# Gate and up products of the feed-forward layers: seven block products with sums of blocks in place of eight

## The chip, the core and the metric

One core of a Trainium2 chip runs the whole program. The metric is the device time of one execution, in microseconds (us). The kernel before was run three times: 1476.43, 1476.70 and 1477.50 us, median 1476.7 us.

## What is computed

A decoder trunk of two layers over 512 tokens of width 1024, in float32. Layer 0 mixes with a gated short convolution, layer 1 with dilated attention; each is followed by the same feed-forward block, which is where the change is. Cut to that:

```python
def swiglu(x, w_gate_up, w_down):          # w_gate_up: 1024 x 5632, w_down: 2816 x 1024
    g, u = jnp.split(x @ w_gate_up, 2, axis=-1)
    return (jax.nn.silu(g) * u) @ w_down

for layer in range(2):
    ...                                    # mixer of the layer
    h = h + rms_norm(y, mix_norm_post[layer])
    f = swiglu(rms_norm(h, ffn_norm_pre[layer]), ...)
    h = h + rms_norm(f, ffn_norm_post[layer])
```

## The kernel before

Every float32 operand of a matrix product is split into a high part (a cast on ACT, L93) and a low part (source minus high part, on DVE, L94). `split` does this. A product is then three matmuls: high times high, low times high, high times low. The weights stand in the array (128 x 128, loaded before each matmul); the activations `xh`, `xl` stream through, 512 token columns at a time (256 in a few places).

`ffn` walks through 11 chunks. A chunk takes 256 gate features and 256 up features; each of the two comes as one load of 1024 x 256 weights (1 MB) into a buffer `raw`, of which there are two. `parts` splits 128 features at a time into `wh` and `wl`, six buffers of each. A chunk is 2 x 2 tiles of 128 features, each 8 blocks of the 1024 inputs times 3 matmuls of 512 columns into one PSUM bank: `feature_mm` (L160) lets a gate tile and an up tile take turns. Afterwards ACT applies silu to the gate bank (L415) and DVE multiplies it with the up bank (L416). `down` follows: 22 blocks of the product's inputs, each 24 matmuls of 512 columns into eight PSUM banks (`y0a` to `y3b`).

The order on each engine is set by a scheduler at build time, which places the instructions of the program by its own estimate of times. Each engine then runs its list strictly in that order: an instruction that waits holds back everything behind it on the same engine. `strict` (L133) pins matmuls to the order in which the program writes them. The attention stage uses it; its products `vps` (values) are matmuls of 256 columns. PSUM has four banks of tag `mm` and four of tag `at`.

The first chunk of `ffn` also finishes the norm of the layer's input: tokens 256 to 511 of `xh` and `xl` are transposed and split during it (`pending.rest`).

Of the kernel before, what the change touches and what calls it, by code (L numbers as in the profile page):

```python
# [15 lines left out]
P = 128  # L16
# [22 lines left out]
def trunk(  # L39
# [27 lines left out]

    xp = [keep.tile([P, KT * T], F32R, name=n, align_bytes=LINE) for n in ("xh", "xl")]  # L70
# [5 lines left out]
    cst = keep.tile([P, 576], F32, name="cst")  # L76
# [5 lines left out]
    cols = keep.tile([P, 64], F32, name="cols")  # L82
    taps, gq, gkv = cols[:, 0:24], cols[:, 24:32], cols[:, 32:40]

    mhalf = keep.tile([P, 1], F32, name="mhalf")
# [2 lines left out]
    def bank(tag, name):  # L88
        return psum.tile([P, T], F32, tag=tag, name=name)
# [14 lines left out]
    def parts(src, gain=None, pool=wp, bufs=6):  # L104


        _, a, b = src.shape
        wh = pool.tile([P, a, b], F32R, tag="wh", name="wh", bufs=bufs, align_bytes=LINE)
        wl = pool.tile([P, a, b], F32R, tag="wl", name="wl", bufs=bufs, align_bytes=LINE)
        if gain is None:  # L110
            split(wh, wl, src)
            return wh, wl
        for i in range(a):
            g = gain[:, i:i + 1]
            nc.scalar.mul(wh[:, i], src[:, i], g)  # L115
            nc.vector.scalar_tensor_tensor(  # L116
                wl[:, i], src[:, i], g, wh[:, i].bitcast(F32), ALU.mult, ALU.subtract)
        return wh, wl
# [272 lines left out]
                    after.after_half(tt, n)  # L391
        return after

    def ffn(layer, pending, after):
        w = ffn_w_gate_up[layer]
        with ExitStack() as phase:
            apool = phase.enter_context(tc.tile_pool(name=f"a{layer}", bufs=4))
            act = []
            for n, bufs in ((1, NF - 12), (0, 12)):
# [3 lines left out]
                act = [pool.tile([P, T], F32, tag=f"act{k}", name="act")  # L403
                       for k in range(bufs)] + act
            for c in range(NF // 2):
                rg = load_cols(w, c * 256)
                ru = load_cols(w, DFF + c * 256)
                mg, mu = makers("mm", rg), makers("at", ru)
                rest = pending.rest() if c == 0 else {}
                if c == 1:  # L410
                    rest["marks"] = [pending.made[NT - 1]] * 4
                ps = feature_mms([mg[0], mu[0], mg[1], mu[1]], **rest)
                for j in range(2):
                    s = apool.tile([P, T], F32, tag="silu", name="s", bufs=2)
                    nc.scalar.activation(s, ps[2 * j], AF.Silu)  # L415
                    nc.vector.tensor_tensor(act[2 * c + j], ps[2 * j + 1], s, ALU.mult)  # L416
# [6 lines left out]
            return down(apool, act, ffn_w_down[layer], held_pool, after)  # L423

    def norm_pool(stack, n):

# [4 lines left out]
    with ExitStack() as phase:  # L431
# [57 lines left out]
        for c in range(KT // 2):  # L489
# [58 lines left out]
    pending = ffn(0, pending, lambda ys: Next(npool, ys, ffn_norm_post[0], None))  # L548

# [299 lines left out]
            f()  # L849

    with ExitStack() as phase:
        npool = norm_pool(phase, 1)
# [31 lines left out]
        ffn(1, pending, lambda ys: Last(npool, ys, ffn_norm_post[1], None))  # L884


_INS = ["x", "positions", "mix_norm_pre", "mix_norm_post", "ffn_norm_pre", "ffn_norm_post",
# [42 lines left out]
```

## Time and profile before

| | before |
|---|---|
| median of three runs | 1476.7 us |
| the profiled execution | 1476.04 us |
| its span, first to last instruction | 1474.3 us |
| TensorE (PE) busy | 1459.1 us, 99% of the span |
| weight loads (PEld) busy | 1247.3 us, 85% |
| DVE busy | 692.6 us, 47% |
| ACT busy | 657.8 us, 45% |
| mean granted TensorE clock | 0.996 of full speed |
| DMA | 93 GB/s on average |

The span and the profiled execution differ by 1.7 us, which lie outside the first and the last instruction. Matmuls are pipelined: a matmul's record is longer than the distance to the next one's start, so the time that a matmul costs is read from the distance of starts or from the length of an unbroken stretch, not from its mean duration.

### The profile page before, as it was taken

The numbers are of one execution on the slowest core, as the hardware profiler recorded it, in microseconds if no ns is written. First come the engines' busy times: TensorE is split into PE (matmuls) and PEld (weight loads), VectorE is DVE, ScalarE is ACT, GpSimd is POOL, SyncE is SP. The second block draws the span as 40 slices with busy tenths as digits, with TensorE's granted clock in tenths as the row PEclk, the third lists the DMA queues.
The fourth block names the chain that finished last, engine by engine and source line by source line (L and its number), as shares of the span: only waits on it lengthen the run. The fifth ranks groups of instructions, "written<-read, shape, count | busy, mean of one in ns | idle before, by whom it ended". The sixth has DMA issues, their size and how long they took to land.

```text
span 1474.3 us, 20308 instructions
## 1 busy us (share of the span) xinstructions
PE 1459.1 (99%) x8160; PEld 1247.3 (85%) x8160; DVE 692.6 (47%) x1381; ACT 657.8 (45%) x1337; POOL 57.3 (4%) x108
## 2 busy tenths in 40 slices
PE   9999999999999999999999999999999999999998
PEld 7888898888888889898899889889789888888886
DVE  5644453232223446767457555745545323223433
ACT  4313342222222336896677768768444222222321
POOL 1000100000000010010000001001010000000000
PEclk9999999999999999999999999999999999999999
DMA  6333123233232312322212312312113331332311
GB/s 217 114 116 114 57 91 107 89 114 103 83 127 102 116 56 70 125 66 92 94 46 87 111 62 60 115 58 60 58 58 115 114 110 62 114 128 94 107 57 57
DMA packets 110516, 137.44 MB, mean 93 GB/s; under 512 B 3502, under 2 KB 99286, under 8 KB 110423
## 3 DMA queue, kind: packets, MB, share of 16 engines
q1 hardware_dynamic: 108852, 135.69, 28.0%
q8 instruction: 64, 1.05, 0.3%
q0 software_dynamic: 1280, 0.26, 0.3%
q14 instruction: 30, 0.24, 0.1%
q10 hardware_dynamic: 290, 0.20, 0.0%
HBM read 133.92 MB, written 2.23 MB: 92 GB/s over the span
## 4 chain that ended last, share of the span: by engine, by line
PE 72%; issue 25%; DVE 1%; POOL 1%; ACT 1%; DMA 0%; SPq 0%; POOLq 0%; DVEq 0%; ACTq 0%
PE mmf L133 16%; PE atf L160 15%; PE mmf L160 12%; PE vps L133 10%; PE s L133 2%; PE tr L133 2%; PE o L133 2%; PE y L133 1%; PE tr L283 1%; PE y2b L231 0%; PE y3b L231 0%; PE y2b L227 0%; PE y3b L227 0%; PE y3b L229 0%; PE y2a L231 0%
## 5 line engine op out<-in xcount | busy, mean ns | idle before, releaser
L94 DVE TENSOR_TENSOR wl<-raw,wh 128x1024 fp32r<-128x1024 f32 x176 | 210.7, 1223 | 70.1 <-ACT wh L93 69.7
L93 ACT CAST wh<-raw 128x1024 fp32r<-128x1024 f32 x176 | 178.1, 1046 | 75.9 <-PE atf L160 43.1
L160 PE MATMUL atf<-xh,wh 128*128 128x512 f32 (+1 forms) x560 | 181.0, 366 | 0.0
L160 PE MATMUL atf<-xh,wl 128*128 128x512 f32 (+1 forms) x560 | 180.4, 365 | 0.0
L160 PE MATMUL atf<-xl,wh 128*128 128x512 f32 (+1 forms) x560 | 180.0, 365 | 0.0
L415 ACT ACTIVATE s<-mmf 128x512 f32<-128x512 f32 x44 | 26.3, 598 | 330.3 <-PE mmf L160 322.1
L416 DVE TENSOR_TENSOR act<-atf,s 128x512 f32<-128x512 f32 x44 | 30.4, 692 | 297.3 <-ACT s L415 297.3
L116 DVE SCALAR_TENSOR_TENSOR wl<-raw,cols,wh 128x256 fp32r<-128x256 f32 x272 | 115.8, 483 | 104.2 <-ACT wh L115 104.2
L160 PE MATMUL mmf<-xh,wh 128*128 128x512 f32 (+1 forms) x496 | 162.1, 365 | 0.6 <-ACT xh L93 0.6
L160 PE MATMUL mmf<-xl,wh 128*128 128x512 f32 (+1 forms) x496 | 160.4, 362 | 0.0
L160 PE MATMUL mmf<-xh,wl 128*128 128x512 f32 (+1 forms) x496 | 160.3, 362 | 0.0
L115 ACT ACTIVATE wh<-raw,cols 128x256 fp32r<-128x256 f32 x272 | 115.0, 498 | 65.5 <-PE mmf L133 46.9
L160 PEld LDWEIGHTS atf<-xh,wh 128*128 128x128 f32 x560 | 99.6, 189 | 16.7
L160 PEld LDWEIGHTS atf<-xh,wl 128*128 128x128 f32 x560 | 99.6, 189 | 16.8
L160 PEld LDWEIGHTS atf<-xl,wh 128*128 128x128 f32 x560 | 99.5, 189 | 16.9
L133 PE MATMUL mmf<-xh,wh 128*128 128x512 f32 x352 | 110.7, 396 | 0.0
L133 PE MATMUL mmf<-xh,wl 128*128 128x512 f32 x352 | 108.8, 390 | 0.0
L133 PE MATMUL mmf<-xl,wh 128*128 128x512 f32 x352 | 108.5, 390 | 0.0
L160 PEld LDWEIGHTS mmf<-xh,wh 128*128 128x128 f32 x496 | 88.6, 191 | 15.6 <-ACT xh L93 1.1
L160 PEld LDWEIGHTS mmf<-xl,wh 128*128 128x128 f32 x496 | 87.5, 189 | 14.4
L160 PEld LDWEIGHTS mmf<-xh,wl 128*128 128x128 f32 x496 | 87.5, 189 | 14.3
L93 ACT CAST ah<-act 128x512 fp32r<-128x512 f32 x44 | 27.1, 620 | 117.5 <-PE y3b L229 116.0
(202 smaller groups left out, 2455.8 us busy)
## 6 DMA issues: line engine op xcount, KB each, us to landing
raw<-in_ffn_w_gate_up SPq DMA_DIRECT2D x44, 1024.0 KB, 6.6
raw<-in_w_kv SPq DMA_DIRECT2D x24, 1024.0 KB, 5.2
raw<-in_ffn_w_down SPq DMA_DIRECT2D x22, 1024.0 KB, 4.8
raw<-in_w_q SPq DMA_DIRECT2D x12, 1024.0 KB, 5.1
raw<-in_conv_w_in SPq DMA_DIRECT2D x11, 1024.0 KB, 5.3
raw<-in_conv_w_out SPq DMA_DIRECT2D x4, 1024.0 KB, 4.9
raw<-in_w_o SPq DMA_DIRECT2D x4, 1024.0 KB, 5.1
h<-in_x SPq DMA_DIRECT2D x4, 512.0 KB, 7.3
```

The costliest lines, as they stand in the source:

```text
L93: return [nc.scalar.copy(hi, src).ins, nc.vector.tensor_tensor(lo, src, hi.bitcast(F32), ALU.subtract).ins]
L94: nc.vector.tensor_tensor(lo, src, hi.bitcast(F32), ALU.subtract).ins]
L115: nc.scalar.mul(wh[:, i], src[:, i], g)
L116: nc.vector.scalar_tensor_tensor(wl[:, i], src[:, i], g, wh[:, i].bitcast(F32), ALU.mult, ALU.subtract)
L133: traced[:] = [op(*args, **kwargs).ins]
L160: nc.tensor.matmul(*args, **kwargs)
L283: nc.tensor.transpose(ps[:, k, :], hn[:, c][:, k * P:(k + 1) * P], ident)
L415: nc.scalar.activation(s, ps[2 * j], AF.Silu)
L416: nc.vector.tensor_tensor(act[2 * c + j], ps[2 * j + 1], s, ALU.mult)
```

## The change

From the third chunk on, in both layers, the product of a weight matrix (1024 inputs x 256 features) with the activations (1024 inputs x 512 tokens) is cut into 2 x 2 blocks: two halves of the inputs, two tiles of 128 features, two halves of the tokens. Eight block products are needed in the plain way. The change forms sums of weight blocks and of activation blocks and gets the same result from seven block products (Winograd's form of Strassen's algorithm), then from sums of the results. A block product is 4 blocks of inputs times 3 matmuls of 256 columns (`product`).

A `Pair` is one load (256 gate or 256 up features), so a chunk is a gate pair and an up pair, and nine chunks in two layers make 36 pairs. In a pair, `parts(n1)` splits the first tile (products 1 and 2), `dh`, `dl` split a block of the second tile (product 4), four additions on DVE overwrite `raw` with sums, and two more `parts` split those (products 6, 3, 7, 5). The results go through three banks: `z` takes products 1, 6, 7 and 4 one on top of the other, and is copied out between them; `zx` takes product 2; `zy` products 5 and 3. Products 4 and 3 of a pair are issued during the next pair. In the last pair of a layer the order differs, so that all ends there.

`sums_of_x` forms the sums of the activation blocks once per layer, in the buffers of the last four `act` tiles, and splits them; one of them, for product 4, replaces a block of `xh`, `xl` in place. The norm's pool is closed during the products and opened again before `down`. `xh`/`xl` and `wh`/`wl` become halves of one tile, `x` and `w`.

The core of the diff:

```diff
-        wh = pool.tile([P, a, b], F32R, tag="wh", name="wh", bufs=bufs, align_bytes=LINE)
-        wl = pool.tile([P, a, b], F32R, tag="wl", name="wl", bufs=bufs, align_bytes=LINE)
+        w = pool.tile([P, 2 * a, b], F32R, tag="w", name="w", bufs=bufs, align_bytes=LINE)
+        wh, wl = w[:, 0:a], w[:, a:2 * a]
...
+    class Pair:
+        def __init__(self, pool, raw, xs, gate, act):
...
+            n1, n2 = raw[:, :, 0:P], raw[:, :, P:2 * P]
+            k1, k2 = slice(0, KT // 2), slice(KT // 2, KT)
...
+            a1 = parts(n1)
+            a22 = [pool.tile([P, KT // 2, P], F32R, tag="ah", name=n, align_bytes=LINE)
+                   for n in ("dh", "dl")]
+            split(*a22, n2[:, k2])
+            add(n2[:, k2], n2[:, k1], n2[:, k2])
+            add(n2[:, k1], n1[:, k1], n2[:, k1])
+            add(n1[:, k1], n1[:, k1], n2[:, k2])
+            add(n1[:, k2], n1[:, k2], n1[:, k1])
+            s1 = parts(n1)
+            s2 = parts(n2)
...
+        def p1(self):
+            self.product(self.z, 1, True, True)
+            nc.scalar.copy(self.r[:, 0:256], self.z)
+        def p2(self):
+            self.product(self.x, 2, True, True)
+            nc.vector.tensor_tensor(self.r[:, 0:256], self.x, self.r[:, 0:256], ALU.add)
+        def p6(self):
+            self.product(self.z, 6, False, True)
+            nc.scalar.copy(self.r[:, 256:512], self.z)
+        def p5(self):
+            self.product(self.y, 5, True, True)
+        def p7(self):
+            self.product(self.z, 7, False, True)
+            nc.scalar.mul(self.r2, self.z, -1.0)
+        def c22(self):
+            nc.vector.tensor_tensor(self.r2, self.r2, self.y, ALU.subtract)
...
+        def p4(self):
+            self.product(self.z, 4, False, True)
...
+        def p3(self):
+            self.product(self.y, 3, False, True)
+            nc.vector.tensor_tensor(self.r[:, 256:512], self.y, self.r[:, 256:512], ALU.add)
...
-            for c in range(NF // 2):
-                rg = load_cols(w, c * 256)
-                ru = load_cols(w, DFF + c * 256)
+            for c in range(2):
+                rg, ru = loads(c)
...
+                xs = sums_of_x(sums, act[-4:])
+                before = None
+                for c in range(2, NF // 2):
+                    gate = None
+                    for raw in loads(c):
+                        p = Pair(apool, raw, xs, gate, act[c])
+                        p.p1()
+                        if gate and c == NF // 2 - 1:
+                            before.p4()
+                            p.p6()
+                            before.p3()
+                            p.p7()
+                            p.p2()
+                            p.p5()
+                            p.c22()
+                            p.p4()
+                            p.p3()
+                            break
+                        p.p2()
+                        if before:
+                            before.p4()
+                        p.p6()
+                        if before:
+                            before.p3()
+                        p.p5()
+                        p.p7()
+                        p.c22()
+                        before = gate = p
```

On PE, a chunk of the kernel before reads like this; a gate and an up tile take turns, and every row is one matmul of 512 columns:

```order
L160 MATMUL mmf<-xh,wh 128x512
L160 MATMUL atf<-xh,wh 128x512
L160 MATMUL mmf<-xh,wl 128x512
L160 MATMUL atf<-xh,wl 128x512
L160 MATMUL mmf<-xl,wh 128x512
L160 MATMUL atf<-xl,wh 128x512
```

The same place in the changed kernel; from product 6 of one pair to product 2 of the next, the `zy<-x` row being product 3 of the pair before:

```order
L134 MATMUL z<-xs,w 128x256 x12
L134 MATMUL zy<-x,w 128x256 x12
L134 MATMUL zy<-xs,w 128x256 x12
L134 MATMUL z<-xs,w 128x256 x12
L134 MATMUL z<-x,w 128x256 x12
L134 MATMUL zx<-x,w 128x256 x12
```

Twelve matmuls of 256 columns now go into one bank in a row, and 84 of them make a pair where 48 of 512 columns did.

On ACT, at the end of a layer's second chunk, the kernel before goes on with silu and the casts of the next chunk's weights:

```order
L415 ACTIVATE s<-mmf 128x512 [waits PE_49,Activation_49]
L93 CAST wh<-raw 128x1024 [waits DMAHW4_49]
L93 CAST wh<-raw 128x1024 [waits DMAHW5_49,PE_49]
L93 CAST ah<-act 128x512 [waits DVE_49]
L415 ACTIVATE s<-mmf 128x512 [waits PE_49,Activation_49]
```

In the changed kernel the same place, where the first pair begins; the first cast is the one that replaces a block of `x`, L440 is the copy of `z` after product 1 of the first pair:

```order
L94 CAST x<-act 128x2x512 [waits PE_49]
L536 ACTIVATE s<-mmf 128x512 [waits PE_49,Activation_49]
L94 CAST w<-raw 128x1024 [waits DVE_49]
L94 CAST w<-raw 128x1024 [waits PE_49]
L440 COPY r<-z 128x256 [waits PE_49]
```

The two casts ahead of the copy are those of the second pair's sums; they stand in front of a copy that the first pair's product 6 needs.

ACT again, in the changed kernel, at the last two pairs of a layer; L455 takes product 7 of the gate pair out of `z`, the four casts are the last pair's two sums and `down`'s first two weights, L462 is a silu, L440 the copy after product 1 of the last pair:

```order
L455 ACTIVATE r_3815<-z 128x256 [waits PE_49,Activation_49]
L94 CAST w<-raw 128x1024 [waits DVE_49]
L94 CAST w<-raw 128x1024
L94 CAST w<-raw 128x1024 [waits DMAHW4_49]
L94 CAST w<-raw 128x1024 [waits Activation_49]
L462 ACTIVATE s_3908<-r_3815 128x256 [waits DVE_49]
L440 COPY r<-z 128x256 [waits PE_49]
```

In the pairs ahead of it three casts stand there, not four.

## Rows read from the trace of the kernel before

**Rows 1.** The page: span, and busy time with its share and instructions.

```profile
span 1474.3 us, 20308 instructions
PE 1459.1 (99%) x8160; PEld 1247.3 (85%) x8160; DVE 692.6 (47%) x1381; ACT 657.8 (45%) x1337; POOL 57.3 (4%) x108
```

**Rows 2.** What PE waited for: us in total, times, longest.

```profile
PE tr L133 <- DVE p L755: 3.4, 1, 3.4
PE s L133 <- DVE st L669: 1.8, 3, 0.6
PE idle L468 <- DVE u L502: 1.3, 1, 1.3
PE tr L283 <- DVE hn L272: 1.3, 2, 1.1
PE mmf L160 <- ACT xh L93: 0.6, 2, 0.3
```

**Rows 3.** Chain that ended last: start, length, unbroken matmuls (first 256 columns, second 512).

```profile
26.81 5.76 PE mmf L160 x48
49.61 10.88 PE mmf L160 x48
...
650.98 17.47 PE vps L133 x144
```

**Rows 4.** Timeline of PE: start, length; eight 256-column matmuls each into one bank.

```profile
193.78 1.12 PE L160 MATMUL mmf<-xh,wl 128*128 128x256 f32 x8
194.74 1.12 PE L160 MATMUL mmf<-xl,wh 128*128 128x256 f32 x8
```

**Rows 5.** Busy time of each engine in one chunk of layer 0.

```profile
239.58:261.30 21.72, 21.72 (x98) 17.98 (x96) 6.71 (x7) 5.48 (x7) 0.00 (x0) 1.00 0.31 98
```

**Rows 6.** Groups by line and shape: count, busy us, mean ns, idle before.

```profile
L94 DVE TENSOR_TENSOR wl<-raw,wh 128x1024 fp32r<-128x1024 f32 x176 | 210.7, 1223 | 70.1 <-ACT wh L93 69.7
L116 DVE SCALAR_TENSOR_TENSOR wl<-raw,cols,wh 128x256 fp32r<-128x256 f32 x272 | 115.8, 483 | 104.2 <-ACT wh L115 104.2
...
L133 PEld LDWEIGHTS vps<-wh,xl 128*128 128x128 f32 x384 | 59.9, 192 | 0.0
...
L755 DVE TENSOR_SCALAR p<-p,f 128x256 f32<-128x256 f32 x112 | 31.9, 352 | 0.0
...
L94 DVE TENSOR_TENSOR al<-act,ah 128x512 fp32r<-128x512 f32 x44 | 30.2, 691 | 98.0 <-ACT ah L93 98.0
L93 ACT CAST ah<-act 128x512 fp32r<-128x512 f32 x44 | 27.1, 620 | 117.5 <-PE y3b L229 116.0 <-DVE act L416 1.5
...
L741 ACT COPY v<-vps 32x256 f32<-32x256 f32 x64 | 23.2, 363 | 0.8
```

**Rows 7.** Timeline of ACT and DVE in a chunk: two casts, two subtractions back to back.

```profile
229.41 1.99 ACT L93 CAST wh<-raw 128x1024 fp32r<-128x1024 f32 x2
...
230.48 2.36 DVE L94 TENSOR_TENSOR wl<-raw,wh 128x1024 fp32r<-128x1024 f32 x2 [0.24 <-ACT wh L93]
```

**Rows 8.** DMA issues: count, KB, median us from issue to landing.

```profile
raw<-in_ffn_w_gate_up SPq DMA_DIRECT2D x44, 1024.0 KB, 6.6
raw<-in_w_kv SPq DMA_DIRECT2D x24, 1024.0 KB, 5.2
raw<-in_ffn_w_down SPq DMA_DIRECT2D x22, 1024.0 KB, 4.8
```

**Rows 9.** Timeline of ACT: the second silu of the second chunk, layers 0 and 1.

```profile
239.80 0.60 ACT L415 ACTIVATE s<-mmf 128x512 f32<-128x512 f32 x1 [7.88 <-PE mmf L160]
...
1151.95 0.60 ACT L415 ACTIVATE s<-mmf 128x512 f32<-128x512 f32 x1 [7.88 <-PE mmf L160]
```

**Rows 10.** PE's longest wait, and busy times with granted clock (1.00 is full) after it.

```profile
1045.48 1.97 PE L133 MATMUL tr<-ident,p 128*128 128x128 f32 x8 [3.37 <-DVE p L755]
...
1045.00:1050.00 5.00, 4.52 (x18) 3.93 (x19) 5.00 (x21) 1.17 (x2) 0.00 (x0) 0.66 0.63 210
```

More of the change, by code (lines that the diff above doesn't have):

```diff
@@ L75, in trunk @@
     ident = keep.tile([P, P], F32, name="ident")
-    cst = keep.tile([P, 576], F32, name="cst")
+    cst = keep.tile([P, 514], F32, name="cst")
     invf, sgn = cst[:, 0:1], cst[:, 1:2]
@@ L392, in down, with add, product @@
         return after
-    def ffn(layer, pending, after):
+    class Pair:
+        def __init__(self, pool, raw, xs, gate, act):
+            self.pool, self.xs, self.gate, self.act = pool, xs, gate, act
+            n1, n2 = raw[:, :, 0:P], raw[:, :, P:2 * P]
+            k1, k2 = slice(0, KT // 2), slice(KT // 2, KT)
+            def add(out, a, b):
+                nc.vector.tensor_tensor(out, a, b, ALU.add)
+            a1 = parts(n1)
[8 more added lines that the diff above has]
+            s2 = parts(n2)
+            self.w = {
+                1: [z[:, k1] for z in a1], 2: [z[:, k2] for z in a1],
+                6: [z[:, k1] for z in s1], 3: [z[:, k2] for z in s1],
+                7: [z[:, k1] for z in s2], 5: [z[:, k2] for z in s2], 4: a22}
+            self.z, self.x, self.y = (bank(t, n)[:, 0:T // 2] for t, n in (
+                ("mm", "z"), ("mm", "zx"), ("at", "zy")))
+            self.r = pool.tile([P, T], F32, tag="al", name="r", align_bytes=LINE)
+            self.r2 = pool.tile([P, T], F32, tag="al", name="r2", align_bytes=LINE)[:, 0:T // 2]
+        def product(self, out, n, first, last):
+            w, x = self.w[n], self.xs[n]
+            out = out.rearrange("p (t n) -> p t n", n=P)
+            for k in range(KT // 2):
+                for p in range(3):
+                    strict(nc.tensor.matmul, out, w[p == 1][:, k, :], x[p == 2][:, :, k, :],
+                           start=first and k + p == 0, stop=last and k == KT // 2 - 1 and p == 2,
+                           skip_group_check=True)
+        def p1(self):
[14 more added lines that the diff above has]
+            nc.vector.tensor_tensor(self.r2, self.r2, self.y, ALU.subtract)
+            g = self.gate
+            if g is None:
+                self.s2 = self.pool.tile([P, T], F32, tag="silu", name="s2", bufs=2)
+                nc.scalar.activation(self.s2[:, 256:512], self.r2, AF.Silu)
+            else:
+                nc.vector.tensor_tensor(
+                    self.act[:, 768:1024], self.r2, g.s2[:, 256:512], ALU.mult)
+        def p4(self):
+            self.product(self.z, 4, False, True)
+            g = self.gate
+            if g is None:
+                nc.scalar.activation(self.s2[:, 0:256], self.z, AF.Silu, scale=-1.0)
+            else:
+                nc.vector.scalar_tensor_tensor(
+                    self.act[:, 512:768], self.z, -1.0, g.s2[:, 0:256], ALU.mult, ALU.mult)
+        def p3(self):
+            self.product(self.y, 3, False, True)
+            nc.vector.tensor_tensor(self.r[:, 256:512], self.y, self.r[:, 256:512], ALU.add)
+            g = self.gate
+            if g is None:
+                self.s1 = self.pool.tile([P, T], F32, tag="silu", name="s1", bufs=2)
+                nc.scalar.activation(self.s1, self.r, AF.Silu)
+            else:
+                nc.vector.tensor_tensor(self.act[:, 0:512], self.r, g.s1, ALU.mult)
@@ new lines, in block, with sums_of_x @@
+    def block(z, k, t):
+        return z[:, 2 * t:2 * t + 2, 4 * k:4 * k + 4, :]
+    def sums_of_x(pool, scratch):
+        b11, b12, b21, b22 = (t.rearrange("p (t k n) -> p t k n", t=2, n=P) for t in scratch)
+        for out, k, t in ((b11, 0, 0), (b12, 0, 1), (b22, 1, 1), (b21, 1, 0)):
+            nc.vector.tensor_tensor(
+                out, *(block(z, k, t).bitcast(F32) for z in (xh, xl)), ALU.add)
+        nc.vector.tensor_tensor(b11, b11, b12, ALU.subtract)
+        nc.vector.tensor_tensor(b12, b22, b12, ALU.subtract)
+        nc.vector.scalar_tensor_tensor(b22, b11, -1.0, b22, ALU.mult, ALU.subtract)
+        nc.vector.scalar_tensor_tensor(b21, b22, -1.0, b21, ALU.mult, ALU.subtract)
+        homes = pool.tile([P, 6 * D], F32R, name="xs", align_bytes=LINE).rearrange(
+            "p (c e t k n) -> p c e t k n", c=3, e=2, t=2, n=P)
+        homes = [[homes[:, c, e] for e in range(2)] for c in range(3)]
+        xs = {n: [block(z, k, t) for z in (xh, xl)]
+              for n, k, t in ((1, 0, 0), (2, 1, 0), (3, 1, 1), (4, 0, 1))}
+        for n, src in ((6, b22), (5, b11), (7, b12), (4, b21)):
+            if n not in xs:
+                xs[n] = homes.pop()
+            split(*xs[n], src)
+        return xs
@@ L395, in ffn @@
+    def ffn(layer, pending, norms, after):
         w = ffn_w_gate_up[layer]
@@ L415, in ffn @@
                     nc.scalar.activation(s, ps[2 * j], AF.Silu)
-                    nc.vector.tensor_tensor(act[2 * c + j], ps[2 * j + 1], s, ALU.mult)
+                    nc.vector.tensor_tensor(
+                        act[c][:, j * T:(j + 1) * T], ps[2 * j + 1], s, ALU.mult)
+            norms.close()
+            with tc.tile_pool(name=f"sums{layer}", bufs=1, side="right") as sums:
+                xs = sums_of_x(sums, act[-4:])
[26 more added lines that the diff above has]
+                        before = gate = p
+            npool = norm_pool(norms, f"{layer}f")
             def held_pool():
@@ L421, in held_pool @@
                 return stack.enter_context(tc.tile_pool(name=f"held{layer}", bufs=2))
-            return down(apool, act, ffn_w_down[layer], held_pool, after)
+            halves = [a[:, j * T:(j + 1) * T] for a in act for j in range(2)]
+            return down(apool, halves, ffn_w_down[layer], held_pool, lambda ys: after(npool, ys))
     def norm_pool(stack, n):
```

18 lines of the change are left out of this document (11 added, 7 removed).

## The prediction

> **What bounds the kernel now.** I read the page first: PE is busy for 1459.1 of 1474.3 us [rows 1]. Then what PE waited for: five causes, 8.4 us together, none of them in the chunks that change [rows 2]. In one such chunk PE is busy for all of its 21.72 us, DVE for 6.71 and ACT for 5.48 [rows 5]. So the time is the sum of the matmuls, and the changed stretch gets shorter by what its matmuls save, until another engine can't keep up. DVE and ACT have room, but the change spends most of it.
>
> **What a matmul costs** is the distance of starts in an unbroken stretch, since the records overlap. 48 matmuls of 512 columns take 10.88 us, 48 of 256 columns 5.76 [rows 3], so 226.7 and 120.0 ns: half the columns cost 53%, not half. The change writes twelve times in a row into one bank. That costs nothing extra: eight matmuls of 256 columns into one bank start 0.96 us ahead of the next eight into it, 120 ns each [rows 4]. In a longer run, 144 in 17.47 us, it is 121.3 ns [rows 3].
>
> **Term 1, the matmuls.** A pair had 48 of 512 columns, 10.88 us; it gets 84 of 256 columns, 84 x 0.120 = 10.08 us. Eight products become seven (12.5% less), but the price of the shorter matmul takes back nearly half of that. 36 pairs x 0.80 = **28.8 us saved**. At 121.3 ns it would be 36 x (10.88 - 10.19) = 24.8.
>
> A weight load stands ahead of each of these matmuls, and its record takes 192 ns [rows 6], longer than the 120 ns from one matmul to the next; in that row of 256-column products the loads lie beside the matmuls.
>
> **Term 2, DVE and ACT inside the pairs.** DVE per pair, by mean durations [rows 6]: three subtractions of 1024 (1.223), one of 512 and four additions of 512 (0.691 each) = 7.1 us, then its sums of results. No row shows a 256-wide sum of two tiles; 0.352 and 0.483 us are the nearest on either side, and I take 0.43, halfway between, to be an estimate. A gate pair has three of these, an up pair four, one of 0.48 and one of 0.69: 1.3 and 2.9 us. A chunk is 18.4 of 20.16 us. Back to back these overlap by a tenth (two subtractions 2.36 us, two casts 1.99) [rows 7], so about 16 us. ACT needs about 11 of 20.16. Neither is the bound by its sum.
>
> What can bound is the strict order. I followed one chunk through ACT's and DVE's lists, with a pair as a slot of 10.08 us, its products each 1.44 us long and seen by the other engines 0.2 us after their last matmul began to drain. Two loops are tight. (a) At the end of a gate pair ACT takes product 7 out of `z` (at 10.28), casts the next pair's two sums and the weights after those (three casts 0.95 us apart), a silu, and only then copies product 1 of the up pair, done at 14.02 us; product 6 of that pair wants the bank at 14.40. Margin 0.4 us. (b) In the up pair the sum after product 3 waits for PE until 17.48, two additions, the same three casts, and then product 7 leaves `z` at 22.3; the next pair's product 4 wants it at 23.04. Margin 0.7 us. The last of the three casts waits for a load as well: its buffer is freed at 14.0, the cast's turn is at 21.0, and loads of this shape that run alone take 5.2 us [rows 8]; the 6.6 of the gate and up loads come from two that start together. Margin 1.8 us. So I take nothing for the inside of the pairs, and keep 0.3 us a chunk, 18 x 0.3 = 5 us, as the upper bound of what small unseen gaps make; below zero nothing is to be had, since PE is already taken as unbroken.
>
> **Term 3, the start of a layer's pairs.** The second chunk ends on PE where its last silu starts, at 239.8 us in layer 0 [rows 9]. Then ACT may cast the block that replaces one of `x` (1.05 us, to 240.9), and DVE, whose list holds the same step, subtracts (to 242.1), makes two additions (to 243.4), and only then can ACT cast the second pair's sums (to 245.3) and reach the copy of product 1 (to 245.65). Product 6 wanted `z` at 239.6 + 2.9 = 242.5. **3.2 us** of waiting. In layer 1 the second chunk ends at 1151.7, one addition less lies in the chain, and the same count gives **2.6 us**. The sums of `x` themselves (eight steps of 1.2 us and four splits, some 15 us of DVE per layer) lie beside the second chunk, 21.7 us of PE with 6.7 of DVE [rows 5]; if that cover were gone they would be late by up to their own length, but by my count they end 4 us or more ahead of the first product that reads them.
>
> **Term 4, the end of a layer's pairs.** There four casts, not three, stand ahead of the copy after the last pair's product 1, and that pair's order takes product 2 out from between: product 6 wants `z` at 12.96 instead of 14.40. The copy is done at 10.55 + 4 x 0.95 + 0.4 (silu) + 0.4 = 15.0. **2.0 us** of waiting. Later DVE, which has `down`'s first subtractions in its list, reads `zy` 0.7 us too late for product 3 of this pair. **2.7 us a layer.** After that `down` has 5.4 us of matmuls for each block and nothing on the path.
>
> **The clock.** Ahead of PE's one wait of 3.37 us it had been little busy, and in the 5 us behind the granted clock was 0.66, that is 1.7 us of full-speed time lost [rows 10]; the shorter waits of [rows 2] left none of this on the page. Four waits of 2.0 to 3.2 us come in; each may cost between 0 and 1.7 us. I take 0.8 us in all, half of one such drop, since PE is dense right up to each wait.
>
> **The sum.** 28.8 - 3.2 - 2.6 - 2 x 2.7 - 0.8 = 16.8 us. The profiled execution of 1476.04 us (span 1474.3) becomes 1459.2, and since it lies 0.7 us below the median of the runs, 1476.7, that becomes **1459.9, say 1460 us**.
>
> **The rivals.**
>
> *Nothing waits at the ends* (0.08): if the copies at the start and the end come sooner than I count them, terms 3 and 4 go and 28.8 us remain: 1448. For it: PE had almost no wait before [rows 2]. Against it: the list on ACT, where the casts stand ahead of the copy whatever they take.
>
> *The margins inside the pairs don't hold* (0.20): loops (a) and (b) have 0.4 and 0.7 us, and each strings together five or six instructions on two engines. If each of six steps costs 0.13 us more than I took, 0.8 us together, (a) is 0.4 us late and (b) 0.1: 18 x 0.5 = 9 us, so 1469; 1467 to 1473 for a little less or more. Against it: durations in the groups hardly vary, and the overlaps were read from this stage [rows 7].
>
> *The weights come too late* (0.08), the one that ends slower: with two buffers, a pair's load can start only when the pair two before has split its sums, at 14.0 in a chunk, and ACT's cast of it at 21.0 stands ahead of the step that frees `z`. The load has 1.8 us in hand over 5.2, and loop (b) 0.7 more. From a landing time of 7.7 us on, each us more is paid once per chunk, 18 times; the kernel is slower by more than 0.2%, 1479.7, from 7.7 + 19.7 / 18 = 8.8 us on. At 9.0 us it would be 18 x 1.3 = 23 us on top of 1460: 1483. Against it: 4.8 to 6.6 us in the rows [rows 8], and fewer loads at a time than before. With a landing of 8.5 to 8.8 us it would end within 0.2% (0.03).
>
> *The weight loads show* (0.01). If a load could not lie beside a matmul at 256 columns, each of the 3024 matmuls would cost up to 192 + 120 ns, 943 us in place of the 392 of before: about 2030 us. The rows speak against it: 120 ns with a load ahead of each [rows 3, 4, 6]. The Trainium skill's page "TensorE: Matmul & The Clock Gate", section "Part 3: Packing small matmuls — row/col tiling", says that weight loads overlap running matmuls only when they go to another group of rows, which full 128-row loads never do; by that rule this rival would be the forecast. The trace does not agree with it here.
>
> That the change does not do what it says I give nothing: PE's list has 3024 matmuls of 256 columns where 1728 of 512 were.
>
> **How the numbers follow.** Forecast, 0.60: 1460, with 1453 to 1467 for the bounds of the price per matmul (4 us), of the clock (up to 6 us more, 1 less) and of terms 3 and 4 (a third either way, 4 us). Margins 0.20, no waits 0.08, late weights 0.08 and 0.03, loads 0.01. The range of 1450 to 1472 leaves out most of the full gain, some of the margins' upper end, and the slow cases: 0.2. Within 0.2% means 1473.7 to 1479.7 us, about what a measurement of this kernel can tell from no change. Faster by more: 0.60 + 0.20 + 0.08 = 0.88; within: 0.03; slower: 0.08 + 0.01 = 0.09.
>
> **What would show it.** Term 1: an unbroken stretch of 12 matmuls `z` in 1.44 us, and a chunk of 20.2 us. Term 2: no wait of PE on ACT or DVE between the fourth and the tenth chunk; if loop (a) fails, PE's `z` waits for L440, if (b), for L455. Terms 3 and 4: one wait of `z` for L440 of 3.2 and 2.6 us about 3 us behind each second chunk, one of 2.0 for L440 and one of 0.7 for DVE's L458 ahead of each `down`. Clock: below 1.00 behind these waits or not. I am wrong if a chunk takes over 20.6 us, or if the loads of single pairs take longer than 7 us to land.

## The result, and the profile after

| | before | after |
|---|---|---|
| time of the runs, median (lowest to highest), us | 1476.57 (1476.35 to 1477.5), 4 runs | 1453.29 (1453.15 to 1455.22), 4 runs |
| ratio, 95% interval | | 0.9844, 0.9827 to 0.9861 |
| profiled execution, time and span, us | 1476.04, 1474.3 | 1453.27, 1451.5 |

The change saves 23.3 us, 1.6%. The forecast was 1460 with a range of 1450 to 1472: the direction and the range are right, and the time is 6.7 us lower than forecast. The page of the profile after the change, its head and its line on the loads of the gate and up weights (count, size, median us from issue to landing):

```profile
span 1451.5 us, 23433 instructions
PE 1433.4 (99%) x9456; PEld 1286.6 (89%) x9456; DVE 913.6 (63%) x1747; ACT 760.4 (52%) x1543; POOL 59.7 (4%) x108
...
raw<-in_ffn_w_gate_up SPq DMA_DIRECT2D x44, 1024.0 KB, 5.1
```

Against [rows 1], PE has 25.7 us less work and is as full as before (99%), while DVE has taken on 221 us and ACT 103. The loads land in 5.1 us where [rows 8] had 6.6. What PE waited for (us in total, times, longest), to be held against [rows 2]:

```profile
PE z L134 <- ACT r L440: 4.0, 2, 2.0
PE tr L134 <- DVE p L909: 3.4, 1, 3.4
PE s L134 <- DVE st L823: 1.8, 3, 0.6
PE idle L622 <- DVE u L656: 1.3, 1, 1.3
PE mmf L161 <- ACT x L94: 0.6, 2, 0.4
PE mmf L161 <- DVE w L95: 0.3, 1, 0.3
```

Two lines are new. `z` waits for ACT's copy L440 twice, 2.0 us each: once in each layer, at the end of its pairs. And a matmul of layer 1's first chunk waits 0.3 us for a low part of a weight. The second to the fifth line stood there before. No line tells of a wait between the first and the last pair. Two stretches of 20.16 us, from the start of layer 0's third chunk on, in the columns of [rows 5]:

```profile
240.10:260.26 20.16, 20.16 (x169) 20.13 (x168) 11.78 (x16) 10.74 (x18) 0.00 (x0) 1.00 0.16 53
260.26:280.42 20.16, 20.16 (x170) 20.16 (x170) 16.93 (x26) 10.18 (x17) 0.00 (x0) 1.00 0.32 105
```

From one pair's product 2 to that of the next pair but one it is 20.16 us in the trace, a chunk, and PE is busy for all of it, where [rows 5] had 21.72. DVE's part grew from 6.71 to 16.93, ACT's from 5.48 to 10.18.

Runs of one kernel differ by up to 4.4 us here, with the granted clock (below). Losses of 1 or 2 us are therefore read between starts of matmuls in the traces. Three stretches carry all that follows: A, from layer 0's first pair to layer 1's first chunk; B, layer 1's first two chunks; C, from layer 1's first pair to the last matmul of the program.

| kernel | median of the runs | A | B | C |
|---|---|---|---|---|
| before | 1476.57 | 865.50 | 46.66 | 315.29 |
| after | 1453.29 | 853.27 | 47.75 | 303.43 |
| x_read_late | 1455.31 | 855.41 | 47.74 | 305.57 |
| p2_back | 1450.57 | 851.85 | 47.75 | 301.95 |
| casts_late | 1451.18 | 851.72 | 47.73 | 302.16 |
| sums_late | 1454.07 | 854.73 | 46.65 | 303.67 |
| layer0_only | 1465.42 | 854.73 | B and C: 361.95 (before 361.95) | |
| pad512 | 1461.30 | 856.52 | 47.74 | 306.99 |
| pad2x512 | 1470.15 | 862.26 | 47.75 | 312.84 |
| short_p2 | 1446.59 | 849.84 | 47.75 | 300.07 |
| all3 | 1447.49 | 851.06 | 46.65 | 301.06 |

So the change gains 12.23 us in A and 11.86 in C, and loses 1.09 in B. If nothing were lost, A and C would each gain the 14.40 of 18 pairs at 0.80.

### The profile page after: what moved, and what is told of

It is laid out like the page before. It is cut to its first block, busy times and chain, and to the rows that moved or that the text cites. A ratio compares the mean times of both kernels' runs of the same rounds, so it can differ in the third digit from the quotient of the medians.

```text
span 1451.5 us, 23433 instructions
## 1 busy us (share of the span) xinstructions
PE 1433.4 (99%) x9456; PEld 1286.6 (89%) x9456; DVE 913.6 (63%) x1747; ACT 760.4 (52%) x1543; POOL 59.7 (4%) x108
## 4 chain that ended last, share of the span: by engine, by line
PE 95%; issue 2%; ACT 1%; DVE 1%; POOL 1%; POOLq 0%; DVEq 0%; ACTq 0%
PE mmf L134 17%; PE z L134 14%; PE vps L134 10%; PE atf L161 10%; PE zy L134 7%; PE mmf L161 7%; PE zx L134 4%; PE s L134 2%; PE o L134 2%; PE tr L134 2%; PE y L134 1%; PE tr L284 1%; PE y0a L230 1%; PE y1b L232 1%; PE y0a L232 1%
## 5 line engine op out<-in xcount | busy, mean ns | idle before, releaser
L95 DVE TENSOR_TENSOR w<-raw,w 128x1024 fp32r<-128x1024 f32 x212 | 251.6, 1220 | 81.7 <-ACT w L94 81.4
L94 ACT CAST w<-raw 128x1024 fp32r<-128x1024 f32 x212 | 212.7, 1046 | 107.3 <-PE atf L161 43.1
L134 PE MATMUL mmf<-x,w 128*128 128x512 f32 x1056 | 246.5, 391 | 0.0
L134 PEld LDWEIGHTS mmf<-x,w 128*128 128x128 f32 x1056 | 196.2, 188 | 39.4
L161 PE MATMUL atf<-x,w 128*128 128x512 f32 (+1 forms) x816 | 174.7, 340 | 0.0
L161 PEld LDWEIGHTS atf<-x,w 128*128 128x128 f32 x816 | 134.9, 190 | 16.8
L134 PE MATMUL vps<-w,x 128*128 128x256 f32 x1152 | 142.3, 284 | 0.0
L134 PEld LDWEIGHTS vps<-w,x 128*128 128x128 f32 x1152 | 139.0, 192 | 1.9
L161 PE MATMUL mmf<-x,w 128*128 128x256 f32 (+1 forms) x624 | 131.3, 326 | 1.0 <-ACT x L94 0.6
L134 PE MATMUL z<-xs,w 128*128 128x256 f32 x864 | 115.8, 284 | 4.0 <-ACT r L440 4.0
L161 PEld LDWEIGHTS mmf<-x,w 128*128 128x128 f32 x624 | 99.3, 191 | 11.5 <-ACT x L94 1.3
```

Of the source, the lines that this page charges most:

```text
L94: return [nc.scalar.copy(hi, src).ins, nc.vector.tensor_tensor(lo, src, hi.bitcast(F32), ALU.subtract).ins]
L95: nc.vector.tensor_tensor(lo, src, hi.bitcast(F32), ALU.subtract).ins]
L134: traced[:] = [op(*args, **kwargs).ins]
L161: nc.tensor.matmul(*args, **kwargs)
```

## The experiments

**x_read_late: when may the cast into `x` begin?** The prediction had put 5.8 us of waiting at the start of the pairs, and the profile shows none. In the trace ACT casts the block that replaces one of `x` at 234.41, well ahead of the second chunk's end at 240.10 (timeline of ACT: start, length, operation):

```profile
234.41 1.05 ACT L94 CAST x<-act 128x1024 fp32r<-128x1024 f32 x1
```

What it overwrites are the input blocks 0 to 3 of two token tiles. The chunk's matmuls go through the input blocks in order, so their last readers are done halfway through the chunk's second pair of features. The experiment reads the blocks in reverse order in that one pair.

```diff
-        todo = [(k, p) for k in range(KT) for p in range(3)]
+        todo = [(k, p) for k in (reversed(range(KT)) if late else range(KT)) for p in range(3)]
...
-                feature_mm(pairs[i:i + 2], 0, NT, attn, fill)
+                feature_mm(pairs[i:i + 2], 0, NT, attn, fill, late and i == 2)
...
-                    rest["marks"] = [pending.made[NT - 1]] * 4
+                    rest.update(marks=[pending.made[NT - 1]] * 4, late=True)
```

> The second chunk's second pair of features reads the eight input blocks in reverse order, so blocks 0 to 3 are read last, and ACT's cast of a sum of x into the place of x's blocks 0 to 3 has to wait for the chunk's end. All else is as in the changed kernel. Theory A: term 3 of the prediction was wrong in one place only, the moment from which this cast may begin (it ran at 234.41, halfway through that pair, not at 240.1). Then it must now start at about 240.3, and with it everything that stands behind it on ACT (a silu, two casts, the copy L440) comes some 1.1 to 1.3 us too late for product 6: a wait of PE of 1.1 to 1.3 us about 3 us behind each second chunk, 2.4 us in all, near 1455.7. Rival B, the chain as the prediction counted it, with DVE's subtraction and two additions in it: waits of 3.2 and 2.6 us, 5.8 in all, near 1459. Rival C, this cast does not set that copy at all: no wait, 1453.3.

Measured: the wait appears in both layers. Timelines of ACT, DVE and PE in x_read_late (in brackets the idle time ahead and what ended it); the second chunk ends at 240.32 here:

```profile
240.07 1.05 ACT L94 CAST x<-act 128x1024 fp32r<-128x1024 f32 x1 [5.22 <-PE atf L161]
...
243.40 0.37 ACT L440 COPY r<-z 128x256 f32<-128x256 f32 x1
...
236.52 1.42 DVE L407 TENSOR_TENSOR raw<-raw 128x512 f32<-128x512 f32 x2
241.15 1.23 DVE L95 TENSOR_TENSOR x<-act,x 128x1024 fp32r<-128x1024 f32 x1 [3.22 <-ACT x L94]
...
243.87 1.67 PE L134 MATMUL z<-xs,w 128*128 128x256 f32 x12 [0.51 <-issue]
```

The cast now waits for PE, and product 6 starts 0.67 us later than two products behind the chunk's end (240.32 + 2.88 = 243.20), of which the profile lists 0.51. Theory A is right in its place and nearly twice too large: the copy L440 comes 3.08 us behind the chunk's end where it came 2.41 behind it, so ACT's list moved by 0.67 and not by 1.05, because the cast overlaps the last matmuls. That all of the 0.67 shows tells that the changed kernel had no room left here. The same place there, timelines of DVE, ACT and PE:

```profile
236.00 1.22 DVE L95 TENSOR_TENSOR x<-act,x 128x1024 fp32r<-128x1024 f32 x1
237.14 1.41 DVE L407 TENSOR_TENSOR raw<-raw 128x512 f32<-128x512 f32 x2
...
242.51 0.38 ACT L440 COPY r<-z 128x256 f32<-128x256 f32 x1
...
242.99 1.67 PE L134 MATMUL z<-xs,w 128*128 128x256 f32 x12
```

The copy ends 0.10 us ahead of product 6 in both.

Rival B, the chain of the prediction, is not tested by this run. With the edit the scheduler also changed DVE's list: in the changed kernel the subtraction stands ahead of the two additions (236.00, 237.14), here behind them (241.15, 236.52). ACT's two casts of the second pair's sums read what these additions write. So with the changed kernel's own list a cast at 240.07 would have held them back; by the distances in these traces product 6 would then have come some 2.9 us late, an estimate that no run checks. That ACT does wait for this chain is seen in pad512, below. The rest of what this kernel's profiled execution lost (A +2.14, C +2.14) is the clock, below.

**p2_back and casts_late: the wait at the end of the pairs.** ACT's and PE's timeline there, in the changed kernel, layer 0:

```profile
409.20 3.87 ACT L94 CAST w<-raw 128x1024 fp32r<-128x1024 f32 x4
412.98 0.41 ACT L462 ACTIVATE s<-r 128x256 f32<-128x256 f32 x1
413.29 0.36 ACT L440 COPY r<-z 128x256 f32<-128x256 f32 x1
...
413.70 1.70 PE L134 MATMUL z<-xs,w 128*128 128x256 f32 x12 [2.01 <-ACT r L440]
415.24 1.60 PE L134 MATMUL zy<-x,w 128*128 128x256 f32 x12
```

Four casts, a silu, the copy: product 6 has to wait until `z` is read. It starts 2.16 us later than straight behind product 4; the listed 2.01 is counted from the end of the last matmul's record. Behind the wait its twelve matmuls take 1.54 us, not 1.44: a restart costs 0.1. The first experiment gives PE other work in that time, the second takes two of the four casts out of ACT's list ahead of the copy.

```diff
                         if gate and c == NF // 2 - 1:
+                            p.p2()
                             before.p4()
...
-                            p.p2()
```

> In the last pair of each layer product 2 is put back between product 1 and product 4, as in all other pairs, in place of behind product 7. Theory A: the wait of 2.0 us at the end of a layer's pairs is that of product 6 for the copy of product 1 behind four casts on ACT, so 1.44 us more of matmuls ahead of it leave 0.6 us of it: 2 x 1.44 = 2.9 us less, near 1450.4. Rival B, the casts themselves come late there because DVE's sums or down's loads are late: ACT is then later by as much, and the time stays at 1453.3. Rival C, product 2's sum on DVE now stands in another's way at the start of down: some of the 2.9 us comes back as a wait of y or zy.

Measured: A 1.42 and C 1.48 us shorter, 2.90 together against 2.9 expected; 0.57 us of the wait is left in each layer. Theory A holds.

```diff
-                pool, wk = apool, parts(raw[:, k % 2:k % 2 + 1, :])
+                with behind(copied): pool, wk = apool, parts(raw[:, k % 2:k % 2 + 1, :])
...
-            nc.scalar.copy(self.r[:, 0:256], self.z)
+            return nc.scalar.copy(self.r[:, 0:256], self.z).ins
...
-                        p.p1()
+                        copied[:] = [p.p1()]
```

> down's casts of its weights are held back until the last pair's product 1 has been copied out of z; by ACT's list two casts instead of four then stand between the copy of product 7 and the copy L440. Theory A: the four casts are the whole of the wait of 2.0 us per layer; with two fewer (0.95 us each) the copy comes 1.9 us sooner and 0.1 us of waiting is left: 2 x 1.9 = 3.8 us less, near 1449.5. Rival B: down's first matmuls then come too late, since their weights and their split of act are made two casts later, and PE waits for w at the start of down for up to 2 us: nothing gained, 1453. Rival C: as A for layer 0, but layer 1 has another limit (half, 1451.4).

Measured: A 1.55 and C 1.27 us shorter, 2.8 of the 3.8 expected. Of the 2.16 us by which product 6 came late behind L440, 0.28 are left (it starts at 412.75, straight behind product 4 it would be 412.47), too short for the list, and the next copy on the same list holds up PE too:

```profile
412.34 0.36 ACT L440 COPY r<-z 128x256 f32<-128x256 f32 x1
415.79 0.38 ACT L448 COPY r<-z 128x256 f32<-128x256 f32 x1
...
412.75 1.69 PE L134 MATMUL z<-xs,w 128*128 128x256 f32 x12
416.23 1.70 PE L134 MATMUL z<-xs,w 128*128 128x256 f32 x12 [0.35 <-ACT r L448]
```

The two casts that were held back, and two splits of `act`, now stand ahead of the copy of product 6, and product 7 waits for that. None of the three expectations had this. Down's first matmuls come in time, so rival B falls.

**sums_late: layer 1's first chunk.** B is 1.09 us longer than before, a loss that the prediction's sum doesn't have at all. In DVE's list there, two sums of `x` stand ahead of the last norm of the rows, and PE later waits for a weight (timelines of DVE, POOL and PE, changed kernel):

```profile
1094.56 2.36 DVE L494 TENSOR_TENSOR act<-x 128x1024 f32<-128x1024 f32 x2
1097.37 1.42 DVE L273 SCALAR_TENSOR_TENSOR hn<-h,y,grow 128x512 f32<-128x512 f32 x2 [0.45 <-POOL y L252]
...
1095.95 1.39 POOL L252 TENSOR_TENSOR y<-a,mhalf 128x1 f32<-128x1 f32 x1
...
1101.23 1.21 DVE L95 TENSOR_TENSOR w<-raw,w 128x1024 fp32r<-128x1024 f32 x1
...
1102.50 2.18 PE L161 MATMUL mmf<-x,w 128*128 128x256 f32 x16 [0.33 <-DVE w L95]
```

The sums end at 1096.92, and the norm (L273) then waits 0.45 us more for POOL. Beside the sums POOL's two steps ahead of the norm, L250 and L252, take 1.34 and 1.39 us by the trace, against 0.30 and 0.56 in the kernel before and in sums_late, where DVE is idle during them. So the norm is late by the sums themselves and by a slower POOL; no run separates the two.

```diff
-            nc.vector.tensor_tensor(
+            with behind(mark): nc.vector.tensor_tensor(
                 out, *(block(z, k, t).bitcast(F32) for z in (xh, xl)), ALU.add)
...
-                xs = sums_of_x(sums, act[-4:])
+                xs = sums_of_x(sums, act[-4:], pending.made[NT - 1] if layer else ())
```

> In layer 1 the four first sums of x on DVE (L494) are issued only once all of x is made, where two of them stood ahead of the last norm of the pending layer's rows. Theory A: the 1.09 us that layer 1's first chunk lost come from these two additions of 1024 ahead of the last hn and of a weight's low part; with them moved, first chunk and second chunk take 46.66 us again as before the change, 1.1 us less: 1452.2. Rival B: the loss in the first chunk has another cause (ACT's casts of the sums, the shape of the start) and stays: 1453.3. Rival C: the sums then end too late for the products that read them at the start of the pairs, and PE waits there for xs: more than 1453.3.

Measured: B is 46.65 us, where 46.66 was before the change; theory A holds for this stretch, and nothing waits for the sums later. The runs are not faster (1454.07, 1452.2 expected). In the profiled execution the clock fell behind the wait at layer 0's end, which took 1.46 us in A; why the other three (1453.71 to 1454.32) are no faster, no trace tells. The 1.1 us are shown by the stretch B alone.

**layer0_only: do the layers touch each other?**

```diff
-            for c in range(2):
+            for c in range(NF // 2 if layer else 2):
...
-                xs = sums_of_x(sums, act[-4:])
+                xs = None if layer else sums_of_x(sums, act[-4:])
-                for c in range(2, NF // 2):
+                for c in range(2, 2 if layer else NF // 2):
```

> Block products in layer 0 alone; layer 1 runs its eleven chunks as before the change. Theory: the layers don't touch each other. Layer 0 keeps its gain of 12.0 us (18 pairs at 0.80 less 2.2 at the end), layer 1's first two chunks take 46.66 us again because no sums of x stand on DVE there, and its other nine chunks take 195.84: 1476.6 - 12.0 = 1464.6. Rival: part of layer 0's gain is given back by what stands between the layers (fewer loads in hand, another order at the hand-over): more than 1465.6.

Measured: 1465.42 (1464.19 to 1465.73). From layer 1's first chunk to the end it takes 361.95 us, to the hundredth what the kernel before took, so nothing is carried over. A is 854.73, 1.46 longer than in the changed kernel; that is again the clock behind the wait of 2.01 us, and the run with the highest mean clock is the shortest, 1464.19.

**pad512 and pad2x512: how much room has loop (a)?** By the trace of the changed kernel, ACT's copy L440 ends at 311.91 and product 6 starts at 312.18 (timelines of ACT and PE, in the middle of layer 0's pairs):

```profile
311.55 0.36 ACT L440 COPY r<-z 128x256 f32<-128x256 f32 x1
...
312.18 1.60 PE L134 MATMUL z<-xs,w 128*128 128x256 f32 x12
```

Both experiments put copies that nothing reads between L455 and L440 of each gate pair, one or two of 512 columns.

```diff
-            nc.scalar.mul(self.r2, self.z, -1.0)
+            padded[:] = [nc.scalar.mul(self.r2, self.z, -1.0).ins]
+            for _ in range(0 if self.gate else 1):
+                with behind(padded):
+                    padded[:] = [nc.scalar.copy(self.spare.bitcast(BF16), cos[:, 0:512]).ins]
...
-            nc.scalar.copy(self.r[:, 0:256], self.z)
+            with behind(padded if self.gate else ()):
+                nc.scalar.copy(self.r[:, 0:256], self.z)
```

> One more ACT instruction per gate pair, a copy of 512 columns that nothing reads, between the copy of product 7 (L455) and the next pair's first copy (L440), about 0.52 us of ACT when others follow at once. Theory A: loop (a) of the prediction is what bounds next, with the margin that the trace of the changed kernel shows, 0.27 us. Then in the 16 chunks that are not last of their layer PE waits 0.52 - 0.27 = 0.25 us at product 6 for L440, and at the two ends the wait grows by all of 0.52: 16 x 0.25 + 1.04 = 5.0 us, near 1458. With the margin of the prediction, 0.4, it would be 3.0 us. Rival B: the chunk is elastic (DVE and ACT idle for 8 and 9 us of 20.16), the copy is only late because it has time to be, and nothing is lost but the ends: 1 us. Rival C: loop (b) is reached as well: over 6 us.

> As the run with one copy, with two of them, about 1.04 us. Theory A: 16 x (1.04 - 0.27) + 2.08 = 14.4 us more than the changed kernel, 1467.7, with waits of 0.77 us at product 6 in each chunk; 16 x 0.52 = 8.3 us more than with one copy, since past the margin each us on ACT is a us on PE. Rival B, elastic: 2 us. Rival C: the later start of product 6 pulls the whole of ACT's list along, so the second loop takes part of it back and less than 8 us are added.

The same place with one copy (L460 is the copy; L442 is the former L440):

```profile
309.17 0.61 ACT L460 CAST r<-cos 128x512 bf16<-128x512 f32 x1
309.68 2.94 ACT L94 CAST w<-raw 128x1024 fp32r<-128x1024 f32 x3
...
312.84 0.35 ACT L442 COPY r<-z 128x256 f32<-128x256 f32 x1
```

One copy takes 0.51 us of ACT's list (309.17 to 309.68), and the chunk grows from 20.16 to 20.55: the margin is 0.12 us net, with the 0.1 that a restart costs; product 6 starts 0.06 us behind the end of L442 (at 313.25), so of the 0.27 in the trace only 0.21 was free. Two copies, 1.02 us, make a chunk of 21.08, so past the margin each us on ACT is a us on PE, as theory A said. The distances between the pairs that loop (b) sets stayed at 10.08 us. Fourteen chunks pay, not sixteen; the first of each layer has room. A and C grow by 6.8 us with one copy (5.0 expected) and by 18.4 with two (14.4 expected, and behind the waits at the ends, now 3.0 us, the granted clock fell to 0.66 over 5 us in both layers). With one copy that is past rival C's mark of 6 us, but not by its mechanism, loop (b). The elastic rival is out.

A part of the excess comes from elsewhere: at the start of layer 1's pairs product 6 is late by 0.48 us with one copy and by 0.65 with two, though no copy was added there. Weights landed later (ACT's cast behind its wait for a load starts 13.4 us ahead of the second chunk's end, 15.9 in the changed kernel), and what follows on both lists moved with it. Timelines of DVE, ACT and PE with one copy; L442 is the former L440 again:

```profile
1143.50 1.22 DVE L95 TENSOR_TENSOR x<-act,x 128x1024 fp32r<-128x1024 f32 x1
1144.63 0.69 DVE L407 TENSOR_TENSOR raw<-raw 128x512 f32<-128x512 f32 x1
...
1145.36 1.99 ACT L94 CAST w<-raw 128x1024 fp32r<-128x1024 f32 x2 [0.36 <-DVE raw L407]
...
1147.72 1.66 PE L134 MATMUL z<-xs,w 128*128 128x256 f32 x12 [0.33 <-issue]
```

Subtraction, addition, ACT's two casts (which wait for the addition), the copy, product 6: this is the chain of the prediction's term 3.

**short_p2: what would bound next?** Here product 2 is computed over one of its four input blocks only.

```diff
+            nk = 1 if n == 2 else KT // 2
-            for k in range(KT // 2):
+            for k in range(nk):
```

> Product 2 of every pair runs only over the first of its four input blocks, 3 matmuls in place of 12, so PE has 1.08 us less in each of the 36 pairs and all else stays (the output lacks the other three blocks of that product). It asks what bounds the pairs next. Theory A, from the margins that the traces and the runs with a longer ACT list show (about 0.2 us in loop (a) and 0.4 in loop (b), net of what a restart costs): in each chunk product 6 of the up pair then waits 1.08 - 0.2 + 0.1 = 1.0 us for L440, and product 4 of the next gate pair 1.08 - 0.4 + 0.1 = 0.8 us for L455. Of 2.16 us saved in a chunk only 0.4 are left, the chunk takes 19.75 us in place of 20.16, and the kernel some 7 to 9 us less: about 1445. Rival B, PE stays the bound as its 99% of busy time suggests: 36 x 1.08 = 38.9 us less, 1414. Rival C: DVE's sum of work (18.4 us in a chunk by mean durations) bounds first: a chunk of 18.4 us, 18 x 1.76 = 32 us less, 1421.

Measured: 1446.59, a chunk of 19.81 us. Of 2.16 us that PE has less to do per chunk, 0.35 arrive. The two largest of PE's waits (L441 and L456 are the former L440 and L455):

```profile
PE z L134 <- ACT r L441: 14.2, 16, 2.0
PE z L134 <- ACT r L456: 9.2, 16, 0.6
```

By the distances of starts PE loses 0.96 us of a chunk at the first, loop (a), and 0.86 at the second, loop (b); 1.0 and 0.8 were expected. Theory A holds: both loops stop PE in the same chunk, while DVE is busy for 17.0 us of 20 and ACT for 10.1. What bounds next is neither engine's sum of work but the chain across three engines, and it lies 0.35 us below PE's 20.16.

**all3: the three losses undone together** (the edits of p2_back, casts_late and sums_late).

> The three edits together: product 2 of the last pair in its usual place, down's weight casts behind that pair's first copy, and layer 1's first sums of x behind the last of x. Theory: the two waits at the ends of the pairs (2.01 us, and 0.1 us of restart) and layer 1's 1.09 us are three separate losses. Product 2's own 1.44 us of matmuls now also cover the copy of product 6 (L448) that came 0.35 us late when only the casts were moved. So from the first pair of layer 0 to layer 1's first chunk 2.1 us less than in the changed kernel, layer 1's first two chunks 46.65, and from layer 1's pairs to the end 2.1 us less: 5.3 us in all, 1448.0. With no wait of 2 us left in front of it, the clock has no reason to fall at the ends of the pairs either, so the runs should lie closer together than those of the changed kernel. Rival: down's start, whose weights and splits come later, takes the place of the wait: then only the 2.9 us of product 2 and the 1.1 of the sums are seen, 1449.3, and PE waits for w or ah at the start of down.

Measured: 1447.49 (1447.35 to 1448.59), ratio to the kernel before 0.9807, 0.9793 to 0.9822: 5.8 us less than the changed kernel. PE's waits, all of them:

```profile
PE tr L134 <- DVE p L909: 3.4, 1, 3.4
PE s L134 <- DVE st L823: 1.8, 3, 0.6
PE tr L284 <- DVE hn L273: 1.6, 2, 1.0
PE idle L622 <- DVE u L656: 1.3, 1, 1.3
PE mmf L161 <- ACT x L94: 0.6, 2, 0.4
```

That is the list of [rows 2] again, with none of the change's own. Against the kernel before, A gains 14.44 us and C 14.23, 28.67 together, where the prediction's first term was 28.8; B is 46.65. The runs lie within 1.2 us. It is the fastest of the versions here that compute the whole output.

## Why the prediction was right, and where it was not

**Term 1 (28.8 us): right.** Twelve matmuls of 256 columns take 1.44 us in the new form, 120.0 ns each, as [rows 3, 4] had it, and a pair 10.08. The rival with weight loads that show did not come, nor did the 121.3 ns of the other end.

**Term 2 (nothing inside the pairs): right, by less than it said.** The list has no wait between the first and the last pair. But loop (a) had 0.12 us net and not 0.4, and together the loops leave 0.35 us of a chunk. The distances of starts show that loop (a) gave way once: in layer 1's eighth chunk ACT takes product 7 out of `z` 0.28 us later than elsewhere, product 6 starts 0.05 us behind the end of the copy L440, and the chunk takes 20.31 us. Why ACT is late there stays open. Of the rival with margins that don't hold, which I gave 0.20, the mechanism is real: its 0.8 us more in the loop would have cost some 0.7 us a chunk, an estimate from the 0.12.

**Term 3 (5.8 us at the start of the pairs): wrong, it is nothing, but with no margin.** The failing step is "Then ACT may cast the block that replaces one of `x`", counted from the second chunk's end. The write waits for the last matmul that reads that block, and by the order of the input blocks the cast may begin 5.7 us ahead of the chunk's end (234.41 for 240.10). The chain behind it was read rightly: subtraction, additions, casts of the sums and copy do wait for each other in the changed kernel's lists. It only ran early enough, its additions done at 238.55, to be over before ACT came to the casts. What was left, a silu, two casts and the copy, ended just in time, so when x_read_late moves the cast, 0.67 us of waiting comes, and when the weights land late, 0.48 (pad512). What the whole chain would cost, 3.2 us by the prediction, no run measures. In layer 1 the prediction's own count gives 2.5 and not 2.6. Half of the rival that nothing waits at the ends, which I gave 0.08, came true this way.

**Term 4 (2.7 us a layer): the 2.0 right, the 0.7 not.** The wait is 2.01 in both layers, by the four casts, as p2_back and casts_late show; a restart of 0.1 comes on top. That the forecast's 2.0 agrees so closely is partly luck: its terms, 10.55 + 3.8 + 0.4 + 0.4, add up to 15.15 and not to 15.0, and the silu takes 0.3 us of the list, not 0.4. The 0.7 us for `zy` didn't come, because product 3 of the last pair no longer stands where the code has it. The order holds it back behind down's first matmuls, and DVE's L458 has read `zy` long before (timelines of DVE and PE):

```profile
422.53 0.41 DVE L458 TENSOR_TENSOR r<-r,zy 128x256 f32<-128x256 f32 x1
...
426.77 0.39 PE L228 MATMUL y0b<-w,ah 128*128 128x512 f32 x1
427.00 1.59 PE L134 MATMUL zy<-x,w 128*128 128x256 f32 x12
```

Straight behind product 4, at 422.44, it would have waited for that read, some 0.5 us by these rows.

**The clock (0.8 us): between its bounds, and a lottery.** In the changed kernel's profiled execution the clock stayed at 1.00 behind both waits; in others it fell. The prediction's reason for half a drop does not hold: it says that PE had been little busy ahead of the wait of 3.37 us, but before that wait, too, PE was dense (kernel before, columns of [rows 5]), and its matmuls run on to the wait:

```profile
1035.00:1040.00 5.00, 5.00 (x41) 4.87 (x40) 4.62 (x14) 3.93 (x8) 0.00 (x0) 1.00 0.37 139
```

See the last section.

**Missing from the sum: 1.09 us in layer 1's first chunk.** The prediction asked whether the sums of `x` end in time and not what stands behind them in DVE's list.

Together, from the 28.8: 2.2 in A and 2.5 in C (the two waits with their restarts, and small gaps), 1.1 in B, and 0.3 that layer 0's pairs begin later by (240.10 for 239.76), which is the start of the program and not the change. That leaves 22.7, which is what the trace has to the last matmul (1467.21 to 1444.55). The forecast took off 5.8 for a chain that was over in time, 1.4 for `zy` and 0.8 for the clock, 8.0 in all; it did not see 1.1 in B, 0.7 of restarts and gaps and the 0.3. So it is partly luck that the forecast missed by no more than 6.7 us: the 2.1 us that it overlooked made up for a part of the 8.0 that it took off too much.

## What to carry to other kernels

On an engine that is busy all the time, count the removed matmuls at the measured distance of starts for their new shape; the rest of the work is at the seams, where the order in which another engine's list releases one buffer decides. For each write into a buffer in use, find its last reader in the order of the matmuls and not in the order of the stages. Before a run is taken as the test of a chain, see in its trace that the scheduler left the chain's steps in their order. A chunk without waits can be a fraction of a us from its next bound, and a short extra instruction in the list shows how far.

## What the runs showed of the hardware beyond that

The clock behind a wait of 2 us can stay or fall, in the same program. Layer 0's end in the changed kernel and in x_read_late, the same wait of 2.01 us, the five us behind it (columns of [rows 5]: the length, busy times, then granted clock, DMA share, GB/s), and product 6 itself in x_read_late:

```profile
415.00:420.00 5.00, 5.00 (x44) 5.00 (x43) 1.71 (x3) 2.41 (x5) 0.00 (x0) 1.00 0.91 365
...
415.00:420.00 5.00, 5.00 (x32) 5.00 (x32) 1.19 (x2) 1.97 (x5) 0.00 (x0) 0.67 0.96 390
...
414.58 2.65 PE L134 MATMUL z<-xs,w 128*128 128x256 f32 x12 [2.01 <-ACT r L440]
417.03 2.17 PE L134 MATMUL zy<-x,w 128*128 128x256 f32 x12
```

At 1.00 PE ran at 2.4 GHz throughout; in the stretch at 0.67 it ran for a part at 1.2 GHz. Product 6 took 2.45 us there instead of 1.54, product 3 of the pair before 2.01 instead of 1.44. Such a fall cost 1.46 us in sums_late and in layer0_only (A against the changed kernel) and 1.47 in each layer of x_read_late (2.14 less the 0.67 of its own wait). Of thirteen waits of 2.0 to 3.0 us at the ends of the pairs in seven profiled executions, eight were followed by it; of the four listed waits of 0.3 to 0.6 us in p2_back and casts_late, none. So a wait of 2 us costs about 2.2 or about 3.7 us here, and what decides between them stays open.
